# Right-side buffers on multiples of 64 bytes, later second halves of the first head, sooner block sums, recurrence chunks on alternating column groups

## The chip, the cores and the metric

The kernel runs on one core of one Trainium2 chip. The metric is the device time of one execution in microseconds (us); the times of several executions are given as a median.

## The reference, cut to what matters

One decoder layer over 1024 positions of width 1024, all in float32:

```python
mod = silu(c) @ w_ada + b_ada;  shift, scale, gate = split(mod, 3)
h = rmsnorm(x, norm_g) * (1 + scale) + shift
proj = h @ w_in                                   # 1024 x 8192
q_a, k_a, v_a, z_a, q_b, f_b, i_b, z_b, g_a, g_b = split(proj, cuts)
o_a = dilated_attention(q_a, k_a, v_a, rel_bias) * silu(z_a)       # 8 heads of 64
o_b = hgrn2_recurrence(silu(q_b), f_b, i_b, lb)                    # 8 heads of 128
o_b = rmsnorm(o_b, hgrn_onorm_g) * silu(z_b)
y = sigmoid(g_a) * (o_a @ w_branch_a) + sigmoid(g_b) * (o_b @ w_branch_b)
x = x + gate * (y @ w_out)
out = rmsnorm(x, final_g)
# recurrence, per head:  S_t = diag(f_t) S_{t-1} + (1 - f_t) i_t^T;  o_t = S_t^T q_t
```

The dilated attention is three patterns of distances merged by their softmax denominators; the kernel does it as one causal softmax whose bias depends on the distance alone, so one table row per head, read as a Toeplitz matrix, holds it.

## The kernel before, in words

**Products.** Every large matmul is done in triples: each operand is split in a rounded high part and the rest (`hi`, `lo`, names ending in h and l), and `mm3` (lines 239, 241, 240) adds hi x hi, lo x hi, hi x lo. The projection `h @ w_in` goes by 2 x 2 blocks of `h` (`b11`, `b12`, `b21`, `b22`) and block sums of them (`t1` to `t4`), seven products for a pair of column tiles in the place of eight; PSUM results are copied by ScalarE into `ct` tiles (`keep`, line 327, and the evictions `ev_...`), combined on VectorE, split, and stored to DRAM (`qk_d`, `vq_d`, ...) by DMAs on SyncE's queue (SP). `ct` is a pool of six buffers.

**Stages.** (1) Start: x is loaded, normalised and transposed, `mods` are made, `h` is written block by block (`make_h`, line 651 and 652), and the block sums are made (`block_sum`: a subtract on VectorE, line 674; a cast on ScalarE, line 675; the low part on VectorE, line 224). `tick` (line 680) moves every sum under way one step on and begins another. (2) A stream of projection steps. (3) Attention, eight heads; steps of the stream (`fill`) are put between its pieces so that TensorE has something to do while VectorE and ScalarE do the softmax. (4) Branch a's output product (`oah`, `oal`), (5) the recurrence, eight heads, again with stream steps between, (6) branch b, `w_out` and the last norm (`yh`, `yl`).

**Order.** TensorE's order is written by hand everywhere, and in stage 1 and the first steps of 2 the other engines' too; later a scheduler orders the others. DMAs on GpSimd's queue (POOL) and on SP's are issued in program order of their engine.

**Attention of one head.** `load_head` (line 865) loads from `qk_d` the first 512 positions of `qp`, `k1`, `k2` (`load_half(h, 0)`), the Toeplitz table `toep` (128 x 1024, 512 KB) and the first half of `vq` (`load_value`); after the second score the other halves follow (`load_half(h, 1)`). `score` makes a row block of 128 queries: two matmuls into `pss` (lines 903, 904), VectorE adds the bias and finds the maximum (line 906), ScalarE takes the exponential, VectorE scales (line 911). `turn` transposes the result on TensorE (`pt`, line 921), `value` multiplies with `vq` (line 936). For head 0 two scores (`begin(0)`) are made before the first `turn`.

**Recurrence of one head.** Levels of chunks `hl` = 1, 2, ..., 64: pairs of neighbouring chunks are joined by products `kk^T qq` into `pp`, which land in `amat`. At `hl` up to 16 (`small`, line 1094) every matmul has 32 stationary columns and writes one of four groups of 32 output partitions in turn. At `hl` = 32 (line 1113) sixteen matmuls write the groups 0 and 64 (+32) in turn; at `hl` = 64 (line 1122) eight matmuls all write partitions 0 to 63. ScalarE copies `pp` into `amat` (lines 1116 and 1124).

**Memory.** [...] At the right end the first tile put is `ctp`, so the small tiles there (of 2 or 8 floats) decide the start addresses of what follows: `ct`, the attention's buffers (`qp`, `k`, `toep`, `vq`, `s`, `pth`, `ptl`, `oa`), `oah`, `oal`, `b12`, `xt`, and the recurrence's (`qb`, `kk`, `amat`, `kt`, `yh`, `yl`, ...) start at 32 past a multiple of 64 bytes. `b11`, `b21`, `b22`, `t1` to `t4`, `w_hi`, `w_lo`, `w_raw` lie at the left end, at multiples of 64.

Of the kernel before, what the change touches and what calls it, by code (L numbers as in the profile page):

```python
# [10 lines left out]
F32 = mybir.dt.float32  # L11
# [8 lines left out]
P = 128  # L20
S = 1024
D = 1024
KT = D // P
# [156 lines left out]
def hybrid_layer(ctx: ExitStack, tc: tile.TileContext, x, w_ada, b_ada, w_in, w_branch_a, w_branch_b, w_out,  # L180
# [6 lines left out]
    dram = ctx.enter_context(tc.tile_pool(name="dram", bufs=1, space=DRAM))  # L187
    hctx = ctx.enter_context(ExitStack())
    hpool = hctx.enter_context(tc.tile_pool(name="hpool", bufs=1))
    cctx = ctx.enter_context(ExitStack())  # L190
    ctp = cctx.enter_context(tc.tile_pool(name="ctp", bufs=CT, side="right"))

# [322 lines left out]
    with ExitStack() as st:  # L515
# [1 line left out]
        pm = st.enter_context(tc.tile_pool(name="ps_main", bufs=1, space=PSUM))  # L517
        xt = [sp.tile([P, KT, 512], F32, name=f"xt{th}") for th in range(2)]
        add_blocks(sp, "b12")
        half = sp.tile([P, 2], F32, name="half")  # L520
        nc.gpsimd.memset(half, -0.5)
        scz = sp.tile([P, KT, 2, 32], F32, name="scz")
        nc.gpsimd.memset(scz, 0.0)
        sc = sp.tile([P, KT], F32, name="sc")
        nc.scalar.activation(half[:, 1:2], half[:, 1:2], AF.Sigmoid)
        nc.scalar.activation(sc, sm[:, C_C:C_C + KT], AF.Sigmoid)
        for a in range(2):
# [101 lines left out]
        def turn_late(j):  # L629

            ps = px.tile([P, 512], F32, name="pxt")
            for t in range(4):
                nc.tensor.transpose(ps[:, t * P:t * P + P], xs[4 + t][:, j * P:(j + 1) * P], ident)
            make_h(j, 1, ps)
# [39 lines left out]
            return [lambda: nc.vector.tensor_tensor(to, a, b_, ALU.subtract),  # L674
                    lambda: nc.scalar.copy(hi[:, s], to), lambda: sub(lo[:, s], to, hi[:, s])]

        sums = [(name, c) for name in ("t1", "t3", "t2", "t4") for c in range(2)]
        under_way = []

        def tick():  # L680

            if sums:
                under_way.append(block_sum(*sums.pop(0)))
            for parts in under_way:
                parts.pop(0)()
            while under_way and not under_way[0]:
                under_way.pop(0)
# [106 lines left out]
        first_products(2, (1,))  # L794
        tick()
        turn_late(3)
        first_products(3, (0,))
        mod_rows(2)
        first_products(3, (1,), (0,))
        mod_turn(2)  # L800
        for n in range(3, 6):
            split_first(n)
        first_products(3, (1,), (1,))
        mod_rows(3)
        first_products(3, (1,), (2,))
        mod_turn(3)
        tick()
        lx.close()
        add_blocks(hctx.enter_context(tc.tile_pool(name="hpool2", bufs=1, reuse_waits="tile")),
                   "b21", "b22", "t2", "t3")  # L810
        stream.issue()
        make_h(4, 0)
        turn_late(4)
        make_h(5, 0)
        first_products(4, (0,))
        turn_late(5)
# [42 lines left out]
    with ExitStack() as at:  # L859
# [7 lines left out]
        def load_head(h):  # L867
            p = h // 2
            if p > 0:
                stream.need(f"qk{p}")  # L870
            while turned.get(("v", p)) != 2:
                stream.step()
            qp, k1, k2 = ([ap1.tile([P, 512], F32R, name=f"{n}{c}") for c in range(2)] for n in ("qp", "k1", "k2"))
            toep = ap1.tile([P, S], F32, name="toep")
            heads[h] = qp, k1, k2, toep, [None, None]
            load_half(h, 0)
            nc.gpsimd.dma_start(toep, bass.AP(tensor=toep_d.tensor, offset=toep_d.offset + h * TOEP,
                                              ap=[[1, P], [1, S]]))
            load_value(h, 0)

        def load_half(h, c):
            qp, k1, k2, _, _ = heads[h]
            p, r = h // 2, slice(E * (h % 2), E * (h % 2) + E)
            for dst, n in ((qp, 4 * p), (k1, 4 * p + 2), (k2, 4 * p + 3)):
                for hh in range(2):
                    nc.gpsimd.dma_start(dst[c][E * hh:E * hh + E],
                                        qk_d[n + hh if dst is qp else n][r, half_of(c)].bitcast(F32R))
# [78 lines left out]
                value(*late.pop(0))  # L966

        load_head(0)
        fill.limit = in_gating
        fill.rate = (in_attention - stream.at) * 4 / NH / sum((j + 1) * w for j, w in enumerate(ATT_W))  # L970
        fill(2.0)
        for _ in begin(0):
            fill(0.5)
        for n, (h, j) in enumerate(items):
            nxt = begin(n + 1)
            for m in range(j + 1):
# [61 lines left out]
    with ExitStack() as hg:  # L1038
# [3 lines left out]
        pools["t"] = hg.enter_context(tc.tile_pool(name="ps_tr", bufs=1, **again))  # L1042
        pou = hg.enter_context(tc.tile_pool(name="ps_ou", bufs=2, **again))

        half = g1.tile([P, 8], F32, name="halfh")
        nc.gpsimd.memset(half, -0.5)
        am = g1.tile([P, 8, P], F32, name="amat")
        nc.gpsimd.memset(am, 0.0)
# [32 lines left out]
        def recurrence(h):  # L1081
# [17 lines left out]
            while hl < P:  # L1099
                q4 = qq.rearrange("p (n two t) -> p n two t", two=2, t=hl)  # L1100
                k4 = kk.rearrange("p (n two t) -> p n two t", two=2, t=hl)
                t3 = fq[:, :2 * n].rearrange("p (n two) -> p n two", two=2)
                if hl <= 16:
                    pl = small(2 if hl == 1 else 1)
                    if hl == 1:
                        nc.vector.tensor_tensor(d3, pl[:, :, 0], mask(0), ALU.mult)
                    nc.vector.copy_predicated(d3, mask(1 + LEVELS.index(hl)).bitcast(I32), pl[:, :, 1 if hl == 1 else 0])
                elif hl == 32:
                    pl = pp.tile([P, 512], F32, name="pp")[:, :256]
                    for c in range(8):  # L1110
                        for b in range(2):
                            o = c * P + 64 * b
                            nc.tensor.matmul(pl[64 * b:64 * b + 32, c * 32:c * 32 + 32], kk[:, o:o + 32],
                                             qq[:, o + 32:o + 64], start=True, stop=True)
                    for b in range(2):
                        nc.scalar.copy(am[64 * b:64 * b + 32, :, 64 * b + 32:64 * b + 64],
                                       c3(pl[64 * b:64 * b + 32]))
                else:
                    pl = pp.tile([P, 512], F32, name="pp")
                    for c in range(8):  # L1120
                        o = c * P
                        nc.tensor.matmul(pl[0:64, c * 64:c * 64 + 64], kk[:, o:o + 64], qq[:, o + 64:o + P],
                                         start=True, stop=True)
                    nc.scalar.copy(am[0:64, :, 64:P], c3(pl[0:64]))
                k_end = t3[:, :, 1:2].to_broadcast([P, n, hl])
                nc.vector.tensor_tensor(k4[:, :, 0, :], k4[:, :, 0, :], k_end, ALU.mult)
                q_end = t3[:, :, 0:1].to_broadcast([P, n, hl])
                nc.vector.tensor_tensor(q4[:, :, 1, :], q4[:, :, 1, :], q_end, ALU.mult)
                if fq is tot:
                    tn = g1.tile([P, S // 2], F32, name="totn")  # L1130
                    other = tot, tn
                else:
                    tn = other[0] if fq is other[1] else other[1]
                nc.vector.tensor_tensor(tn[:, :n], t3[:, :, 0], t3[:, :, 1], ALU.mult)
                fq = tn
                n //= 2
                hl *= 2
                yield 2.6
                if hl == 8:
                    load_z(h)  # L1140
                if hl == 32 and h + 1 < NHB:
                    load_f(h + 1)
# [84 lines left out]
    with ExitStack() as mg:  # L1227
# [122 lines left out]
        with ExitStack() as fo:  # L1350
            f1 = fo.enter_context(tc.tile_pool(name="fo1", bufs=1, **right))
            f2 = fo.enter_context(tc.tile_pool(name="fo2", bufs=2, **right))
            half = f1.tile([P, 1], F32, name="halff")
            nc.gpsimd.memset(half, -0.5)
            fg = f1.tile([P, D], F32, name="fg")
            nc.sync.dma_start(fg, final_g.to_broadcast([P, D]))
# [103 lines left out]
```

## Time and profile before

| | |
|---|---|
| median of 3 runs | 1141.77 us (1139.42 to 1144.51) |
| the profiled execution, its own time | 1141.97 us |
| its span in the trace | 1140.2 us |
| mean granted TensorE clock over the span | 0.994 |
| TensorE busy | 1112.2 us, 98% |
| VectorE / ScalarE / GpSimd busy | 71% / 45% / 10% |

The profiled execution lies 0.2 us from the median. A busy TensorE is one with a matmul in flight; a matmul's start and its length overlap with the next one's, so the distance from one start to the next is what a matmul costs.

### The profile page before, as it was taken

What the parts mean: (1) busy time and instruction counts of PE and PEld (TensorE: products, weight loads), DVE (VectorE), ACT (ScalarE), POOL (GpSimd) and SP (SyncE); (2) the same over time, 40 slices, a digit from 0 to 9 for tenths busy, and PEclk for the clock granted to TensorE, in tenths of its full rate; (3) what the DMA queues carried; (4) which work ended last, traced back from release to release, by engine and by line L of the source; (5) the groups of instructions that cost most, each with busy time, mean ns of one, the idle gap of its engine ahead of it and who ended that gap; (6) DMA issues with size and microseconds to landing.
All of it is one profiled execution on the core that took longest, in us unless ns stands there. A gap on an engine that the chain in (4) does not pass through costs nothing.

```text
span 1140.2 us, 21715 instructions
## 1 busy us (share of the span) xinstructions
PE 1112.2 (98%) x8322; PEld 912.8 (80%) x8322; DVE 808.2 (71%) x1607; ACT 516.5 (45%) x1056; POOL 117.2 (10%) x195
## 2 busy tenths in 40 slices
PE   7998999999999999999999999999999999999997
PEld 5677788888888888878887878787887878888886
DVE  4486888878877776844778797878888773769053
ACT  4474555677555555632343444333443432334021
POOL 1102112202202201100000000000000012000000
PEclk9999999999999999999999999999999999999999
DMA  9739476656646624856625254443535379864052
GB/s 321 219 102 252 136 195 181 180 131 163 153 120 162 158 80 139 265 174 195 222 89 173 93 168 140 141 155 107 174 90 181 106 252 328 276 209 140 21 184 74
DMA packets 161480, 189.54 MB, mean 166 GB/s; under 512 B 11312, under 2 KB 107696, under 8 KB 161376
## 3 DMA queue, kind: packets, MB, share of 16 engines
q1 hardware_dynamic: 140080, 153.95, 42.3%
q0 software_dynamic: 20896, 33.60, 12.2%
q8 instruction: 65, 1.06, 0.4%
q10 hardware_dynamic: 400, 0.61, 0.2%
q14 instruction: 39, 0.32, 0.1%
HBM read 129.36 MB, written 58.76 MB: 165 GB/s over the span
## 4 chain that ended last, share of the span: by engine, by line
PE 85%; DVE 6%; DMA 4%; issue 2%; ACT 2%; POOL 1%; SPq 0%; POOLq 0%; DVEq 0%; ACTq 0%
PE m L239 18%; PE m L241 17%; PE m L240 16%; PE pq L240 4%; PE pq L241 4%; PE pq L239 4%; PE po L936 3%; PE pt L921 3%; PE pp L1094 3%; PE pss L904 2%; PE pss L903 1%; PE pou L1177 1%; PE pou L1162 1%; PE pou L1179 1%; PE pxt L640 1%
## 5 line engine op out<-in xcount | busy, mean ns | idle before, releaser
L224 DVE TENSOR_TENSOR w_lo<-w_raw,w_hi 128x512 fp32r<-128x512 f32 x156 | 106.7, 687 | 54.1 <-ACT w_hi L246 48.6
L246 ACT CAST w_hi<-w_raw 128x512 fp32r<-128x512 f32 x146 | 90.5, 620 | 59.9 <-PE m L241 50.3
L327 ACT COPY ct<-m 128x512 f32<-128x512 f32 x90 | 52.6, 585 | 93.7 <-PE m L241 72.0
L246 ACT CAST w_hi<-w_s 128x512 fp32r<-128x512 f32 x90 | 55.9, 621 | 74.0 <-PE m L241 51.0
L274 DVE TENSOR_TENSOR ct<-m,ct 128x512 f32<-128x512 f32 x90 | 61.8, 686 | 26.5 <-PE m L241 26.1
L224 DVE TENSOR_TENSOR w_lo<-w_s,w_hi 128x512 fp32r<-128x512 f32 x90 | 61.8, 687 | 15.2 <-ACT w_hi L246 13.5
L909 ACT ACTIVATE s<-s,st 128x128 f32<-128x128 f32 (+3 forms) x64 | 49.8, 778 | 31.5 <-DVE st L906 31.4
L925 ACT CAST pth<-pt 128x512 fp32r<-128x512 f32 (+1 forms) x80 | 43.6, 544 | 36.5 <-PE pt L921 32.0
L224 DVE TENSOR_TENSOR ptl<-pt,pth 128x512 fp32r<-128x512 f32 (+1 forms) x80 | 50.5, 631 | 7.7 <-ACT pth L925 7.0
L239 PE MATMUL m<-t2h,w_hi 128*128 128x512 f32 x120 | 50.4, 420 | 4.2 <-ACT ct L327 4.2
L1185 POOL TENSOR_TENSOR ssh<-ssh,halfh 128x4 f32<-128x4 f32 x16 | 18.1, 1128 | 345.1 <-DVE ssh L1184 345.1
L239 PE MATMUL m<-b11h,w_hi 128*128 128x512 f32 x124 | 51.6, 416 | 0.0
L239 PE MATMUL m<-b21h,w_hi 128*128 128x512 f32 x124 | 51.2, 413 | 0.0
L239 PE MATMUL m<-b22h,w_hi 128*128 128x512 f32 x124 | 50.8, 410 | 0.0
L239 PE MATMUL m<-t1h,w_hi 128*128 128x512 f32 x120 | 50.3, 419 | 0.5 <-DVE ct L274 0.5
L239 PE MATMUL m<-t4h,w_hi 128*128 128x512 f32 x120 | 49.6, 414 | 0.4 <-DVE ct L274 0.4
L239 PE MATMUL m<-t3h,w_hi 128*128 128x512 f32 x120 | 49.6, 414 | 0.0
L241 PE MATMUL m<-b11l,w_hi 128*128 128x512 f32 x124 | 48.8, 394 | 0.0
L241 PE MATMUL m<-b21l,w_hi 128*128 128x512 f32 x124 | 48.7, 393 | 0.0
L241 PE MATMUL m<-b22l,w_hi 128*128 128x512 f32 x124 | 48.7, 393 | 0.0
L240 PE MATMUL m<-b11h,w_lo 128*128 128x512 f32 x124 | 48.5, 391 | 0.0
L240 PE MATMUL m<-b21h,w_lo 128*128 128x512 f32 x124 | 48.5, 391 | 0.0
(358 smaller groups left out, 3193.8 us busy)
## 6 DMA issues: line engine op xcount, KB each, us to landing
w_raw<-in_w_in_dram SPq DMA_DIRECT2D x128, 256.0 KB, 3.4
wa<-in_w_ada_dram SPq DMA_DIRECT2D x16, 512.0 KB, 8.9
qk_d<-ct SPq DMA_DIRECT2D x32, 256.0 KB, 3.5
k<-qk_d POOLq DMA_DIRECT2D x64, 128.0 KB, 4.9
qp<-qk_d POOLq DMA_DIRECT2D x32, 128.0 KB, 4.9
toep<-toep_d POOLq DMA_DIRECT2D x8, 512.0 KB, 6.5
vq_d<-ct SPq DMA_DIRECT2D x16, 256.0 KB, 3.4
vq<-vq_d POOLq DMA_DIRECT2D x16, 256.0 KB, 4.2
```

The lines of the kernel that those rows point to most:

```text
L224: nc.vector.tensor_tensor(out_, a, hi.bitcast(F32), ALU.subtract)
L239: nc.tensor.matmul(ps, ah, bh, start=start, stop=False, skip_group_check=more)
L240: nc.tensor.matmul(ps, al, bh, start=False, stop=False, skip_group_check=more)
L241: nc.tensor.matmul(ps, ah, bl, start=False, stop=stop, skip_group_check=more)
L246: nc.scalar.copy(hi, src)
L274: nc.vector.tensor_tensor(out_, a, b_, op)
L327: nc.scalar.copy(c[name], b[which])
L909: nc.scalar.activation(s[:, :kw], s[:, :kw], AF.Exp, bias=prev, scale=-1.0, accum_out=st2[:, 2:3])
L921: nc.tensor.transpose(pt[:, c0:c0 + P], pn[b][:, kt * P:(kt + 1) * P], ident)
L925: nc.scalar.copy(pth[:, :w], pt[:, :w])
L936: nc.tensor.matmul(po[:, 256 - n:256], vq[kt // 4][:, kt % 4], src[:, c0:c0 + n], start=kt == 0 and a == 0, stop=kt == 2 * j + 1 and a == 1)
L1094: nc.tensor.matmul(pl[32 * b:32 * b + 32, c], kk[:, o:o + 32], qb[:, 2 - n:2, o:o + 32], start=True, stop=True)
```

## The change

1. A tile of 8 floats, `edge`, is put at the right end ahead of everything, and the small tiles `half`, `sc`, `halfh`, `halff` become 16 floats. The tiles named under Memory then start at multiples of 64 bytes.
2. `toep` is loaded in two halves of 512 columns, each with its `load_half`. For head 0, four copies of one column from the first `vq` tile into the second halves' tiles stand ahead of their loads, so that these are issued after that `vq` has landed.
3. The block sums come in another order, and `tick` is called at other places.
4. The first two scores of head 0 are made sooner in TensorE's order.
5. At `hl` = 32 and 64 neighbouring chunks write different groups of output partitions (four groups, two groups), and the copies to `amat` become four of 32 x 128 and two of 64 x 256.

```diff
+    ctx.enter_context(tc.tile_pool(name="edge", bufs=1, side="right")).tile([P, 8], F32, name="edge")
     ctp = cctx.enter_context(tc.tile_pool(name="ctp", bufs=CT, side="right"))
...
-        sums = [(name, c) for name in ("t1", "t3", "t2", "t4") for c in range(2)]
+        sums = [("t1", 0), ("t1", 1), ("t3", 0), ("t2", 0), ("t3", 1), ("t2", 1), ("t4", 0), ("t4", 1)]
...
-        def tick():
+        def tick(another=True):
-            if sums:
+            if sums and another:
...
         turn_late(3)
+        tick()
         first_products(3, (0,))
...
         mod_turn(2)
+        tick(False)
...
         mod_turn(3)
-        tick()
...
         turn_late(4)
+        tick(False)
...
             load_half(h, 0)
-            nc.gpsimd.dma_start(toep, bass.AP(tensor=toep_d.tensor, offset=toep_d.offset + h * TOEP,
-                                              ap=[[1, P], [1, S]]))
             load_value(h, 0)
...
+            if h == 0 and c == 1:
+                got = heads[h][4][0][:, 0, 0:1].bitcast(F32)
+                for t in (qp[1], k1[1], k2[1]):
+                    nc.gpsimd.tensor_copy(t[:, 0:1], got)
+                nc.gpsimd.tensor_copy(toep[:, 512:513], got)
+            nc.gpsimd.dma_start(toep[:, half_of(c)],
+                                bass.AP(tensor=toep_d.tensor, offset=toep_d.offset + h * TOEP + 512 * c,
+                                        ap=[[1, P], [1, 512]]))
...
         load_head(0)
+        first = begin(0)
...
-        fill(2.0)
-        for _ in begin(0):
-            fill(0.5)
+        for amount in (0.7, 2.3):
+            next(first)
+            fill(amount)
+        next(first, None)
...
-                    pl = pp.tile([P, 512], F32, name="pp")
-                    for c in range(8):
-                        o = c * P
-                        nc.tensor.matmul(pl[0:64, c * 64:c * 64 + 64], kk[:, o:o + 64], qq[:, o + 64:o + P],
-                                         start=True, stop=True)
-                    nc.scalar.copy(am[0:64, :, 64:P], c3(pl[0:64]))
+                    for c in range(8):
+                        for o in range(0, P, 2 * hl):
+                            to = o + hl * (c % 2)
+                            nc.tensor.matmul(pl[to:to + hl, c // 2], kk[:, c * P + o:c * P + o + hl],
+                                             qq[:, c * P + o + hl:c * P + o + 2 * hl], start=True, stop=True)
+                    pairs = am.rearrange("p (c two) t -> p two c t", two=2)
+                    for odd in range(2):
+                        for o in range(0, P, 2 * hl):
+                            nc.scalar.copy(pairs[o:o + hl, odd, :, o + hl:o + 2 * hl],
+                                           pl[o + hl * odd:o + hl * odd + hl])
```

GpSimd's queue at head 0, before the change: the loads of `qp`, `k` (k1 and k2), `toep` and `vq` (`vq_d` is written by the stream).

```order
L886 DMA qp_1007<-qk_d 64x512 x2
L886 DMA k_1009<-qk_d 64x512 x2
L886 DMA k_1011<-qk_d 64x512 x2
L877 DMA toep<-toep_d 128x1024
L886 DMA qp_1008<-qk_d 64x512 x2
L886 DMA k_1010<-qk_d 64x512 x2
L886 DMA k_1012<-qk_d 64x512
L891 DMA vq<-vq_d 128x4x128
L886 DMA k_1012<-qk_d 64x512
L891 DMA vq<-vq_d 128x4x128 x2
```

The same place of the changed kernel:

```order
L891 DMA toep<-toep_d 128x512
L897 DMA qp_1011<-qk_d 64x512 x2
L897 DMA k_1013<-qk_d 64x512 x2
L897 DMA k_1015<-qk_d 64x512 x2
L902 DMA vq<-vq_d 128x4x128 x3
L889 CAST qp_1012<-vq 128x1
L889 CAST k_1014<-vq 128x1
L889 CAST k_1016<-vq 128x1
L890 COPY toep<-vq 128x1
L891 DMA toep<-toep_d 128x512
L897 DMA qp_1012<-qk_d 64x512 x2
L897 DMA k_1014<-qk_d 64x512 x2
```

Ahead of the first `vq` stood eleven loads of `qp` and `k` and the whole `toep`; now there stand six and half a `toep`, and the second halves have moved behind the `vq` loads and the four copies.

ScalarE in stage 1, around the casts of `t1`'s two halves (`row` feeds the transposes of `mods`; `b21h` is a block that TensorE reads next), before:

```order
L652 CAST b12h<-xt_114 128x512
L577 COPY row<-pmod 128x256
L609 CAST w_hi<-w_raw_321 128x512
L609 CAST w_hi<-w_raw_323 128x512
L609 CAST w_hi<-w_raw_325 128x512
L577 COPY row<-pmod 128x256
L675 CAST t1h<-xt_113 128x1024
L651 ACTIVATE xt_113<-xt_113,mods 128x512
L652 CAST b21h<-xt_113 128x512
```

and of the changed kernel:

```order
L654 CAST b12h<-xt_118 128x512
L677 CAST t1h<-xt_117 128x1024
L579 COPY row<-pmod 128x256
L677 CAST t1h<-xt_117 128x1024
L611 CAST w_hi<-w_raw_325 128x512
L611 CAST w_hi<-w_raw_327 128x512
L611 CAST w_hi<-w_raw_329 128x512
L579 COPY row<-pmod 128x256
L653 ACTIVATE xt_117<-xt_117,mods 128x512
L654 CAST b21h<-xt_117 128x512
```

Both casts of `t1h` now stand ahead of the three `w_hi`; none stands between the second `row` and `b21h`.

TensorE at the start of attention, from the second score of head 0 to the first transposes of a softmax (`pt`, line 921), before; the first score stands 8 rows further up:

```order
L903 MATMUL pss<-k_1009,qp_1007 128x256
L904 MATMUL pss<-k_1011,qp_1007 128x256
L239 MATMUL m_888<-t3h,w_hi 128x512
L240 MATMUL m_888<-t3h,w_lo 128x512
L241 MATMUL m_888<-t3l,w_hi 128x512
L239 MATMUL m_888<-t3h,w_hi 128x512
L240 MATMUL m_888<-t3h,w_lo 128x512
L241 MATMUL m_888<-t3l,w_hi 128x512
L921 MATMUL pt<-kc,s_1061 128x128
L921 MATMUL pt<-kc,s_1082 128x128 x2
```

and in the changed kernel, the rows around the two scores:

```order
L243 MATMUL m_912<-b22l,w_hi 128x512
L914 MATMUL pss<-k_1013,qp_1011 128x128
L915 MATMUL pss<-k_1015,qp_1011 128x128
L241 MATMUL m_912<-b22h,w_hi 128x512
L242 MATMUL m_912<-b22h,w_lo 128x512
L243 MATMUL m_912<-b22l,w_hi 128x512
L241 MATMUL m_912<-b22h,w_hi 128x512
L242 MATMUL m_912<-b22h,w_lo 128x512
L243 MATMUL m_912<-b22l,w_hi 128x512
L914 MATMUL pss<-k_1013,qp_1011 128x256
L915 MATMUL pss<-k_1015,qp_1011 128x256
L241 MATMUL m_912<-b22h,w_hi 128x512
```

Between the second score and the first `pt` there are now 27 matmuls of 512 columns in the place of 6; the `pt` rows stand where they stood, and elsewhere TensorE's order is the same.

## Rows read from the trace of the kernel before

**Rows 1.** The page: busy time of each engine.

```profile
PE 1112.2 (98%) x8322; PEld 912.8 (80%) x8322; DVE 808.2 (71%) x1607; ACT 516.5 (45%) x1056; POOL 117.2 (10%) x195
```

**Rows 2.** Timeline of PE, 95 to 106 us: start, length, instruction, idle before and releaser.

```profile
96.48 1.03 PE L447 MATMUL pt<-kc,ct 128*128 128x128 f32 x8
101.68 0.78 PE L239 MATMUL m<-t2h,w_hi 128*128 128x512 f32 x1 [4.16 <-ACT ct L327]
...
105.20 0.39 PE L241 MATMUL m<-t2l,w_hi 128*128 128x512 f32 x1
105.43 0.39 PE L239 MATMUL m<-t2h,w_hi 128*128 128x512 f32 x1
```

**Rows 3.** Windows: us, PE, PEld, DVE, ACT, POOL busy, then PEclk, DMA share, GB/s.

```profile
97.00:101.60 4.60, 0.52 (x5) 0.28 (x3) 1.16 (x2) 0.56 (x2) 0.00 (x0) 1.00 1.05 305
101.60:105.20 3.60, 3.52 (x9) 2.79 (x9) 2.98 (x6) 1.95 (x6) 2.84 (x4) 0.53 0.57 123
```

**Rows 4.** Timeline of ACT, 95 to 106 us.

```profile
101.04 0.59 ACT L327 COPY ct<-m 128x512 f32<-128x512 f32 x1 [4.29 <-DMA vq_d<-ct]
```

**Rows 5.** Timeline of POOL's issues, 84 to 106 us.

```profile
89.00 0.58 POOL L877 DMA_DIRECT2D toep<-toep_d  x1
...
102.11 0.79 POOL L891 DMA_DIRECT2D vq<-vq_d  x1 [9.95 <-ACT ct L327]
```

**Rows 6.** The page's DMA issues: KB each, median us from issue to landing.

```profile
k<-qk_d POOLq DMA_DIRECT2D x64, 128.0 KB, 4.9
...
toep<-toep_d POOLq DMA_DIRECT2D x8, 512.0 KB, 6.5
vq_d<-ct SPq DMA_DIRECT2D x16, 256.0 KB, 3.4
vq<-vq_d POOLq DMA_DIRECT2D x16, 256.0 KB, 4.2
```

**Rows 7.** Timeline of SP's issues, 84 to 106 us.

```profile
94.22 11.49 SPq L453 DMA_DIRECT2D vq_d<-ct  x7
```

**Rows 8.** Timeline of PE, 59 to 62 us.

```profile
61.26 0.50 PE L661 MATMUL pm<-b21h,w_hi 128*128 128x512 f32 x1 [1.06 <-ACT b21h L652]
```

**Rows 9.** Timeline of ACT, 51 to 62 us.

```profile
54.61 0.37 ACT L577 COPY row<-pmod 128x256 f32<-128x256 f32 x1 [2.54 <-PE pmod L574]
...
58.79 1.05 ACT L675 CAST t1h<-xt 128x1024 fp32r<-128x1024 f32 x1
```

**Rows 10.** Timeline of PE, 109 to 125 us.

```profile
115.33 0.30 PE L921 MATMUL pt<-kc,s 128*128 128x128 f32 x1 [0.38 <-DVE s L911]
116.76 0.44 PE L921 MATMUL pt<-kc,s 128*128 128x128 f32 x2 [1.13 <-DVE s L911]
...
124.38 0.49 PE L903 MATMUL pss<-k,qp 128*128 128x512 f32 x1
```

**Rows 11.** Timeline of PE in the first recurrence head: blocks of small matmuls, two records each.

```profile
560.07 1.10 PE L1094 MATMUL pp<-qb,kk 128*32 128x64 f32 x64
...
564.04 0.76 PE L1094 MATMUL pp<-qb,kk 128*32 128x32 f32 x64
...
578.66 0.70 PE L1113 MATMUL pp<-qb,kk 128*32 128x32 f32 x32
...
581.55 1.15 PE L1122 MATMUL pp<-qb,kk 128*64 128x64 f32 x16
```

**Rows 12.** Groups by form on PE, 545 to 995 us: count, busy us, mean ns.

```profile
L241 PE MATMUL m<-b11l,w_hi 128*128 128x512 f32 x60 | 23.6, 394 | 0.0
...
L1122 PE MATMUL pp<-qb,kk 128*64 128x64 f32 x128 | 9.2, 225 | 0.0
```

**Rows 13.** Groups by form on PE, 480 to 560 us.

```profile
L239 PE MATMUL m<-oah,w_hi 128*128 128x512 f32 x64 | 25.5, 398 | 0.0
...
L239 PE MATMUL m<-t2h,w_hi 128*128 128x512 f32 x8 | 3.1, 389 | 0.0
```

**Rows 14.** Groups by form on PE, 990 to 1140 us.

```profile
L240 PE MATMUL pq<-t2h,yl 128*128 128x512 f32 x30 | 12.0, 399 | 0.0
```

More of the change, by code (lines that the diff above doesn't have):

```diff
@@ L519, in hybrid_layer @@
         add_blocks(sp, "b12")
-        half = sp.tile([P, 2], F32, name="half")
+        half = sp.tile([P, 16], F32, name="half")[:, 0:2]
         nc.gpsimd.memset(half, -0.5)
@@ L523, in hybrid_layer @@
         nc.gpsimd.memset(scz, 0.0)
-        sc = sp.tile([P, KT], F32, name="sc")
+        sc = sp.tile([P, 16], F32, name="sc")[:, 0:KT]
         nc.scalar.activation(half[:, 1:2], half[:, 1:2], AF.Sigmoid)
@@ L876, in load_head @@
             load_half(h, 0)
-            nc.gpsimd.dma_start(toep, bass.AP(tensor=toep_d.tensor, offset=toep_d.offset + h * TOEP,
-                                              ap=[[1, P], [1, S]]))
             load_value(h, 0)
         def load_half(h, c):
-            qp, k1, k2, _, _ = heads[h]
+            qp, k1, k2, toep, _ = heads[h]
+            if h == 0 and c == 1:
[6 more added lines that the diff above has]
+                                        ap=[[1, P], [1, 512]]))
             p, r = h // 2, slice(E * (h % 2), E * (h % 2) + E)
@@ L1043, in hybrid_layer @@
         pou = hg.enter_context(tc.tile_pool(name="ps_ou", bufs=2, **again))
-        half = g1.tile([P, 8], F32, name="halfh")
+        half = g1.tile([P, 16], F32, name="halfh")
         nc.gpsimd.memset(half, -0.5)
@@ L1107, in recurrence @@
                     nc.vector.copy_predicated(d3, mask(1 + LEVELS.index(hl)).bitcast(I32), pl[:, :, 1 if hl == 1 else 0])
-                elif hl == 32:
-                    pl = pp.tile([P, 512], F32, name="pp")[:, :256]
+                else:
+                    pl = pp.tile([P, 512], F32, name="pp")[:, :4 * hl].rearrange("p (c t) -> p c t", c=4)
                     for c in range(8):
[L1111 to L1118, printed above, removed]
-                    pl = pp.tile([P, 512], F32, name="pp")
-                    for c in range(8):
-                        o = c * P
-                        nc.tensor.matmul(pl[0:64, c * 64:c * 64 + 64], kk[:, o:o + 64], qq[:, o + 64:o + P],
-                                         start=True, stop=True)
-                    nc.scalar.copy(am[0:64, :, 64:P], c3(pl[0:64]))
+                        for o in range(0, P, 2 * hl):
[7 more added lines that the diff above has]
+                                           pl[o + hl * odd:o + hl * odd + hl])
                 k_end = t3[:, :, 1:2].to_broadcast([P, n, hl])
@@ L1352, in hybrid_layer @@
             f2 = fo.enter_context(tc.tile_pool(name="fo2", bufs=2, **right))
-            half = f1.tile([P, 1], F32, name="halff")
+            half = f1.tile([P, 16], F32, name="halff")[:, 0:1]
             nc.gpsimd.memset(half, -0.5)
```

## The prediction

> **What bounds the kernel now.** The first view is the page's busy times [rows 1]: TensorE has a matmul in flight for 1112.2 of 1140.2 us, so there are two ways to gain, its gaps (28 us in all) and the cost of what it runs. The second view is the timeline of TensorE, where a bracket names a wait. The longest one that the change touches is at 101.68 us: 4.16 us idle, for a copy into a `ct` tile on ScalarE [rows 2]. [...] After that wait the matmuls start further apart: the eight from 101.68 to 105.20 took 3.52 us, where the next one starts 0.23 us after its forerunner. [...] Following the wait back: ScalarE's copy at 101.04 stood still for 4.29 us until a store of `vq_d` had left its `ct` tile [rows 4]; those stores begin to be issued on SP's queue at 94.22 [rows 7], so the first took some 6.8 us, against a median of 3.4 [rows 6]. In that stretch the DMA engines' share is 1.05 and they move 305 GB/s [rows 3]: the store is late because GpSimd's queue is loading all of head 0 beside it, the 512 KB of `toep` issued at 89.00 among it [rows 5]. Last come the views by form, for the lengths of single matmuls.
>
> **The change part by part.** The sum is made against the profiled execution, 1141.97 us, which is 0.2 us above the median.
>
> *Later loads.* Before, eleven loads of `qp` and `k` at 128 KB and a `toep` of 512 KB [rows 6] stand ahead of the first `vq`: 1.9 MB. After, six and half a `toep`: 1.0 MB. With half the load the queue is empty before the stores begin, and I give the store its median: issued at 94.22, landed at 97.6, copied by 98.3 with the 0.59 us of [rows 4]. TensorE runs dry at 97.5 (the row at 96.48 and its 1.03 us), so 0.8 us remain of 4.16, and a wait that short leaves the clock alone: the matmul behind the wait of 1.06 us at 61.26 lasts 0.50 us [rows 8], the one behind 4.16 us 0.78 [rows 2]. The slow matmuls lost 3.52 less 8 x 0.23, 1.7 us. **Gain 3.4 + 1.7, 5.0 us.** Bounds: 0, if the store is late for another reason, and 5.8.
>
> Where the stall goes: the second halves are late next. `vq` is issued when its store has landed, now near 99 us and not 102.11 [rows 5]; at 4.2 us to landing [rows 6] the four copies behind it begin near 103.5. No row prices such a copy; at 0.58 us, the length of an issue [rows 5], they and the seven loads behind them take 6.4 us of GpSimd, and the last load lands, at 4.9 us [rows 6], near 115. The first score that reads a second half stands at 124.38 [rows 10], which the gains ahead of it bring to about 117. They have 2 us to spare; the cost is nothing unless they are later than that, and then what they are later (bounds 0 and 3, at copies of 1 us and loads as slow as the 6.5 us of `toep`). Behind those loads on GpSimd's queue stand only the loads of head 1, due a head later. The other heads' `toep` in two halves is one more issue of some 0.5 us each on a GpSimd that is 10% busy [rows 1]: nothing.
>
> *Sooner sums.* TensorE waits 1.06 us at 61.26 for `b21h` [rows 8], and on ScalarE a cast of `t1h`, 1.05 us, stands ahead of it at 58.79 [rows 9]. It moves up to where ScalarE idled 2.54 us before 54.61 [rows 9]. The other half's cast now stands ahead of the three `w_hi` casts and may push these by 1 us. **Gain 0.9 us**, bounds a loss of 1 and a gain of 1.06. The later sums are named by no wait of TensorE.
>
> *Sooner scores.* The two first transposes of a softmax wait 0.38 and 1.13 us for VectorE's scaling [rows 10]. Ahead of them there were 6 matmuls behind the second score; now there are 27, at 0.23 us 6.2 us of work. **Gain 1.5 us**, bounds 0 and 1.5. What the scores read, the first halves, is issued by the time at which `toep` was before, 89.00, and takes at most the 6.5 us of the whole `toep`: there before 100, when the score comes.
>
> *Column groups.* This is arithmetic on four blocks of the first recurrence head [rows 11]. At 64 columns, sixteen records in one group take 1.15 us, and 64 records in four groups 1.10 us. At 32 columns, 32 records in two groups take 0.70 us, and 64 in four groups 0.76 us. So it isn't the records that cost but the rounds, a round being one matmul in each group: all four blocks have sixteen. With a last matmul of 0.22 us [rows 12], a round is (1.15 - 0.22) / 15, 0.062 us, and (0.76 - 0.22) / 15, 0.036 us. The change makes eight rounds of each: 7 x 0.062 + 0.22 is 0.65 us (0.50 less) and 7 x 0.036 + 0.22 is 0.47 us (0.23 less). I take 0.71 a head for the drain between blocks, over eight heads. **Gain 5.7 us.** Bounds: 0, if groups of 64 and four of 32 at this step don't overlap, and 7.4, if all of 1.15 and 0.70 were halved. [...]
>
> The copies into `amat` become six a head, three more. Each is at most as long as a copy of 512, 0.59 us [rows 4], on an engine 45% busy [rows 1]; ScalarE also makes the `w_hi` that the stream waits for. Bounds 0 and 14 us (24 copies); I take **a loss of 1.0 us**, as if two heads held the stream up by one copy each.
>
> *Alignment.* Of matmuls with 512 columns beside each other, those on `oah` (at 32 past a multiple of 64) last 398 ns, those on `t2h` (at a multiple) 389 [rows 13]; those on `yl` 399 [rows 14]. There are 192 on `oah` and `oal`, 30 on `yl`: 222 x 9 ns, **a gain of 2.0 us**. Bounds: 0, if something else in those rows differs, and some 10 us above that: in the recurrence a matmul with both operands aligned lasts 394 [rows 12], 5 ns over the 389 of the quiet stage, and nothing in the rows says whether the traffic of the misaligned `ct` causes it; 7 products of 3 groups of 60 there and about as many in attention make some 2,400 x 4 ns. I stay with the row that names the tile. [...]
>
> **Sum:** 5.0 + 0.9 + 1.5 + 5.7 - 1.0 + 2.0 = 14.1 us, so 1141.97 - 14.1 = 1127.9.
>
> **The rivals.**
> A. The stall stays: the store is late by the stream's own weight loads, or another `ct` is. For it: a share of 1.05 leaves no room, and it isn't only GpSimd's queue. Against it: GpSimd's part halves. 1127.9 + 5.0 = 1133.
> B. The groups don't overlap in this step. For it: no row shows two groups of 64. Against it: groups of 32 do [rows 11]. 1127.9 + 5.7 = 1133.6. A and B together: 1138.6, no change.
> C. Alignment gives nothing: 1130. Its opposite, C', is that it also frees the aligned matmuls of stages 3 and 5: 1118.
> D. The slower side: going from one column group to another costs, rather than overlaps. Eight heads x (8 + 16) matmuls make 192 such changes. The rest of the sum is a gain of 8.4 us, so from 44 ns each the gain is gone, and from 73 ns each the kernel is slower by 5.7: 1148 at that. For it: a round of 64 columns costs 62 ns alone, so a wait for the end of one of 225 [rows 12] would do it. Against it: blocks with four groups change with every matmul and cost no more.
>
> **How the numbers follow.** What a measurement tells from no change is about 0.5%, 5.7 us. The forecast as summed has 0.45 (1125 to 1131), C 0.15, C' 0.12, A 0.12, B 0.09, A with B 0.04, D 0.03. Leaving out half of C' below, and A with B and D above, the range is 1119 to 1135. Faster by over 0.5% is below 1136: all but the last two and a tail of A and B, 0.84; no change 0.12; slower 0.04.
>
> **What would show it.** Right: the row on `t2h` behind the eight transposes with under 1 us idle and 0.23 us to the next; no wait for `b21h` at 61; none at the first `pt`; blocks of line 1127 of about 0.47 and 0.65 us; `oah` and `yl` at 389. Wrong: a wait of TensorE or VectorE on GpSimd's loads at the fifth score (late second halves), new waits for `w_hi` behind line 1132 in the recurrence, or blocks of 0.7 and 1.15 us as before.

## The result and the profile after

The changed kernel takes 1131.03 us (median of 6 runs, 1129.33 to 1134.70) against 1142.15 of the kernel before (6 runs): a ratio over all these runs of 0.9909, 95% interval 0.9895 to 0.9924, which is 10.4 us less (the two medians by themselves lie 11.1 us apart). The profiled execution took 1134.70 us (span 1132.9) and is the slowest of the six; two of its waits (2.50 and 2.05 us) were shorter when the same kernel was profiled again (0.95 and 0.47 us).

The page's busy times, and TensorE's timeline at the places of [rows 2], [rows 8], [rows 10] and [rows 11]:

```profile
PE 1105.6 (98%) x8322; PEld 908.8 (80%) x8322; DVE 807.6 (71%) x1607; ACT 519.5 (46%) x1080; POOL 123.1 (11%) x207
```

```profile
59.36 0.50 PE L663 MATMUL pm<-b21h,w_hi 128*128 128x512 f32 x1
...
94.57 1.03 PE L449 MATMUL pt<-kc,ct 128*128 128x128 f32 x8
96.73 0.50 PE L241 MATMUL m<-t2h,w_hi 128*128 128x512 f32 x1 [1.13 <-ACT ct L329]
97.07 0.40 PE L242 MATMUL m<-t2h,w_lo 128*128 128x512 f32 x1
...
108.33 0.49 PE L932 MATMUL pt<-kc,s 128*128 128x128 f32 x3
...
115.99 0.48 PE L914 MATMUL pss<-k,qp 128*128 128x512 f32 x1
...
122.17 0.50 PE L914 MATMUL pss<-k,qp 128*128 128x512 f32 x1 [2.50 <-DVE st L917]
...
474.34 0.75 PE L241 MATMUL m<-b11h,w_hi 128*128 128x512 f32 x1 [2.05 <-DVE ct L276]
...
577.07 0.46 PE L1127 MATMUL pp<-qb,kk 128*32 128x32 f32 x32
...
579.73 0.69 PE L1127 MATMUL pp<-qb,kk 128*64 128x64 f32 x16
```

The reader is to see what has gone and what has come. Gone: the wait for `b21h`, the two waits at the first `pt`, 3.0 of the 4.16 us on `t2h` (and the slow clock behind: from 97 to 101 us it is granted 1.00, where behind the wait before it was 0.53 [rows 3], and the next matmul starts 0.34 us later, at 97.07, not 0.58), 0.24 and 0.46 us of the two blocks of the recurrence. Come: 2.50 us at 122.17, where a score waits for VectorE. The row at 115.99, the first to read a second half, has no bracket: the late loads are in time. What they do is seen in ScalarE's timeline and in the windows (columns as in [rows 3]):

```profile
117.62 0.59 ACT L329 COPY ct<-m 128x512 f32<-128x512 f32 x1 [3.32 <-DMA qk_d<-ct]
```

```profile
89.00:92.00 3.00, 3.00 (x16) 2.52 (x15) 2.24 (x4) 2.01 (x6) 0.00 (x0) 1.00 0.41 77
101.00:122.00 21.00, 18.67 (x88) 15.19 (x86) 16.12 (x38) 10.62 (x24) 5.12 (x13) 1.00 0.99 265
...
122.00:126.00 4.00, 3.70 (x13) 2.87 (x14) 2.98 (x11) 2.28 (x5) 0.00 (x0) 0.60 0.41 131
```

A copy into `ct` stands still for 3.32 us again, now under a store of `qk_d`; behind it on ScalarE is a `w_hi`, behind that VectorE's `w_lo`, which stands still for 3.25 us until 118.76, and behind that, in VectorE's order, the score's reduction, at 121.42. From 101 to 122 us the DMA engines' share is 0.99: the second halves (1.0 MB) lie there now, beside weights and stores, while from 89 to 92 us the share is 0.41. Behind the wait the granted clock falls to 0.60. The wait at 474 is behind a load of `ga_d`.

The form rows that answer to [rows 13] and [rows 14]:

```profile
L241 PE MATMUL m<-oah,w_hi 128*128 128x512 f32 x64 | 25.3, 396 | 0.0
L242 PE MATMUL m<-oah,w_lo 128*128 128x512 f32 x64 | 25.3, 395 | 0.0
L243 PE MATMUL m<-oal,w_hi 128*128 128x512 f32 x64 | 25.3, 395 | 0.0
```

```profile
L241 PE MATMUL pq<-t2h,yh 128*128 128x512 f32 x30 | 11.9, 397 | 0.0
L243 PE MATMUL pq<-t2l,yh 128*128 128x512 f32 x30 | 11.8, 394 | 0.0
L242 PE MATMUL pq<-t2h,yl 128*128 128x512 f32 x30 | 11.8, 394 | 0.0
```

Aligned, `oah` still lasts 396 ns and not 389; `yl` went from 399 to 394.

### The profile page after: what moved, and what is told of

Same layout as the page of the kernel before. It is cut to its first block, busy times and chain, and to the rows that moved or that the text cites. A ratio compares the mean times of both kernels' runs of the same rounds, so it can differ in the third digit from the quotient of the medians.

```text
span 1132.9 us, 21754 instructions
## 1 busy us (share of the span) xinstructions
PE 1105.6 (98%) x8322; PEld 908.8 (80%) x8322; DVE 807.6 (71%) x1607; ACT 519.5 (46%) x1080; POOL 123.1 (11%) x207
## 3 DMA queue, kind: packets, MB, share of 16 engines
q8 instruction: 65, 1.06, 0.4%
## 4 chain that ended last, share of the span: by engine, by line
PE 88%; DVE 4%; DMA 3%; ACT 2%; issue 1%; POOL 1%; POOLq 0%; DVEq 0%; ACTq 0%; SPq 0%
PE m L241 18%; PE m L243 16%; PE m L242 16%; PE pq L243 5%; PE pq L242 5%; PE pq L241 5%; PE po L947 3%; PE pt L932 3%; PE pp L1107 3%; PE pss L915 1%; PE pss L914 1%; PE pou L1186 1%; DMA w_raw<-in_w_in_dram 1%; PE pou L1188 1%; PE pm L663 1%
```

## The experiments

The theory after the result: the gain is that of the column groups, the sums and the scores; alignment gives little, and the later loads pay with a new wait for what they take off the old one. The rivals: alignment carries several us all over the kernel; the new wait belongs to the sooner scores; it is a chance of one execution. Ten runs have times enough for an interval; each ratio is to runs of the kernel before beside it (medians 1140.55 to 1142.29):

| run | median, us | ratio to before, 95% interval |
|---|---|---|
| column groups alone | 1136.89 | 0.9957 (0.9942 to 0.9972) |
| sums and scores alone | 1136.81 | 0.9949 (0.9930 to 0.9968) |
| alignment alone | 1140.76 | 0.9989 (0.9972 to 1.0006) |
| later loads alone | 1140.68 | 0.9995 (0.9983 to 1.0008) |
| changed, without alignment | 1135.77 | 0.9931 (0.9904 to 0.9958) |
| changed, old loads | 1130.44 | 0.9893 (0.9874 to 0.9912) |
| changed, again | 1129.93 | 0.9906 (0.9890 to 0.9923) |
| changed, toep and qp at once | 1128.86 | 0.9902 (0.9880 to 0.9924) |
| the same again | 1130.33 | 0.9898 (0.9877 to 0.9918) |
| changed, toep, qp and k1 at once | 1130.45 | 0.9910 (0.9888 to 0.9931) |

The four parts alone multiply to 0.9890; the whole is 0.9909. What the parts give alone is about what they give together.

**Column groups alone.**

```diff
-                        nc.tensor.matmul(pl[0:64, c * 64:c * 64 + 64], kk[:, o:o + 64], ...)
+                            to = o + hl * (c % 2)
+                            nc.tensor.matmul(pl[to:to + hl, c // 2], kk[:, c * P + o:c * P + o + hl], ...)
```

> The kernel before with only the column groups of the recurrence changed (hl = 32 and 64 on alternating groups, six copies). Theory: rounds set the price, blocks of 0.39 and 0.61 us in the place of 0.63 and 1.07, eight heads, so 5.6 us less than before, about 1136.5; the stall of 4.2 us at 101.7 us is still there. Rival: part of what the changed kernel gained in the recurrence came from the buffers' alignment there; then this run gains less than 4.

0.9957 of 1141.48 is 4.9 us (3.2 to 6.6). The timeline of TensorE has the same two blocks as in the changed kernel, with the buffers as before:

```profile
577.44 0.46 PE L1114 MATMUL pp<-qb,kk 128*32 128x32 f32 x32
577.83 0.50 PE L239 MATMUL m<-b22h,w_hi 128*128 128x512 f32 x1
...
580.09 0.69 PE L1114 MATMUL pp<-qb,kk 128*64 128x64 f32 x16
580.71 0.50 PE L239 MATMUL m<-b21h,w_hi 128*128 128x512 f32 x1
```

(The expectation's 0.39 and 0.61 are the distances from a block's first start to the next row's start; the savings are the same by either measure.) So the blocks owe nothing to alignment: 0.24 and 0.46 us less than [rows 11], 5.6 us over eight heads. The whole recurrence says the same: from the first matmul into `pp` to the last it is 372.7 to 372.9 us in the four profiles with the old groups and 367.1 to 367.4 in the nine with alternating ones.

**The same groups without alternation.**

```diff
-                            to = o + hl * (c % 2)
-                            nc.tensor.matmul(pl[to:to + hl, c // 2], ...)
+                            to = o + hl * (c // 4)
+                            nc.tensor.matmul(pl[to:to + hl, c % 4], ...)
```

> The changed kernel, with the same column groups and the same six copies in the recurrence, but neighbouring chunks on the same groups: chunks 0 to 3 on the first, 4 to 7 on the second. Theory (a round is what matmuls on different groups do at once): without alternation sixteen rounds are back, blocks of about 0.63 us at 32 columns and 1.07 at 64. Rival (the price hangs on the count of groups or on the copies, or the engine looks further ahead than its next matmul): blocks of 0.39 and 0.61 us as in the changed kernel.

Neither the theory nor the rival holds. Timed once, 1137.51 us; the timeline, and windows of 0.28, 0.21 and 0.36 us over the 64-column block (PE and PEld busy with the count of records, then clock):

```profile
575.56 0.60 PE L1127 MATMUL pp<-qb,kk 128*32 128x32 f32 x32
...
578.36 0.97 PE L1127 MATMUL pp<-qb,kk 128*64 128x64 f32 x16
```

```profile
578.35:578.63 0.28, 0.27 (x4) 0.27 (x5) 1.00 0.00 0
578.63:578.84 0.21, 0.21 (x11) 0.21 (x9) 1.00 0.00 0
578.84:579.20 0.36, 0.36 (x12) 0.35 (x8) 1.00 0.00 0
```

0.97 lies between 1.15 and 0.69, 0.60 between 0.70 and 0.46. The counts (records in flight in each window) say how: few in the first window, most in the second. There the last records of the first group run beside the first of the second; at both ends one group runs alone. The single records of the trace bear this out: each group has eight, most of them 58 ns apart, and the second group's first starts 0.29 us into the block, beside the first group's fifth. Here matmuls of different groups did overlap without standing next to each other, but only from 0.29 us into the block; alternation is worth the rest, 0.28 of the 0.46 us and 0.14 of the 0.24.

**Sums and scores alone.** The diff's parts on `sums`, `tick`, `begin(0)`; loads, buffers and recurrence as before.

```diff
-        sums = [(name, c) for name in ("t1", "t3", "t2", "t4") for c in range(2)]
+        sums = [("t1", 0), ("t1", 1), ("t3", 0), ("t2", 0), ("t3", 1), ("t2", 1), ("t4", 0), ("t4", 1)]
...
+        first = begin(0)
```

> The kernel before with only the sooner block sums and the sooner first scores, which lie far enough apart to be read separately in one trace. Theory: no wait for b21h near 61 us (0.95 us), none at the first transposes of a softmax (1.9 us), the wait of 4.2 us near 101 us as before: 2.5 us less, 1138.5. Rival: the sooner scores bring a wait of their own near 122 us and the sum is nothing, 1141.

5.8 us less (3.7 to 8.0), twice what was expected. TensorE's timeline:

```profile
59.03 0.50 PE L661 MATMUL pm<-b21h,w_hi 128*128 128x512 f32 x1
...
96.78 0.50 PE L239 MATMUL m<-t2h,w_hi 128*128 128x512 f32 x1 [1.50 <-ACT ct L327]
...
108.32 0.49 PE L923 MATMUL pt<-kc,s 128*128 128x128 f32 x3
```

The two small waits are gone as expected, and no wait follows at 122, which takes the rival away. But in this profile the wait on `t2h` is 1.50 us and no slow clock follows it (granted 1.00 from 96 to 105 us), with the old loads all in place.

**Old loads in the changed kernel.**

```diff
-            nc.gpsimd.dma_start(toep[:, half_of(c)], ...)      # in load_half
+            nc.gpsimd.dma_start(toep, ...)                     # in load_head
```

> The changed kernel with head 0's loads as they were (toep whole, second halves ahead of the first vq). Theory: the wait of about 4 us for a ct tile comes back near 97 us, with the slow clock behind it (5 us in all), and the wait near 122 us (0.9 to 2.5 us in the changed kernel, with up to 1.3 us of slow clock) is gone, so 1 to 4 us more than the changed kernel, 1131 to 1134. Rival (the wait near 122 us belongs to the sooner scores): it is there too, 1135 or more.

The wait is back, and the one at 122 is gone; the time is that of the changed kernel (1130.44 against 1131.03 and 1129.93), a little under what was expected:

```profile
99.98 0.50 PE L241 MATMUL m<-t2h,w_hi 128*128 128x512 f32 x1 [3.50 <-ACT ct L329]
```

```profile
100.00:105.00 5.00, 5.00 (x23) 4.17 (x24) 3.95 (x8) 2.75 (x7) 2.85 (x4) 1.00 0.78 174
```

After 3.50 us idle the granted clock stayed at 1.00; after 4.16 it fell to 0.53 [rows 3]. The two other profiles with the old loads, column groups alone and then alignment alone, have shorter waits than 4.16 and a fall behind each:

```profile
99.92 0.59 PE L239 MATMUL m<-t2h,w_hi 128*128 128x512 f32 x1 [3.84 <-ACT ct L327]
98.83 0.50 PE L241 MATMUL m<-t2h,w_hi 128*128 128x512 f32 x1 [3.09 <-ACT ct L329]
```

```profile
100.00:105.00 5.00, 5.00 (x15) 3.96 (x16) 4.01 (x8) 2.69 (x7) 2.86 (x4) 0.66 0.73 152
100.00:105.00 5.00, 5.00 (x17) 3.92 (x16) 4.02 (x9) 1.60 (x5) 2.11 (x4) 0.67 0.97 201
```

So of five waits with the old loads three have a slow clock behind them (4.16, 3.84 and 3.09 us; granted 0.67, 0.66 and 0.67 from 100 to 105 us) and two don't (3.50 and 1.50; granted 1.00 behind them): in these traces the length of the wait alone doesn't decide it.

The traces also show why moving the loads gives nothing in all. The second profile of the changed kernel (below) has 2.1 us less from the first matmul on `b21h` to the one on `t2h` above than this run (37.67 against 39.75), 1.8 us more from the first score matmul of 512 columns to the eleventh (21.60 against 19.83), and 0.57 us more at the very end: from the last matmul on `yh` to the end of the span it is 6.84 to 6.85 us in the five profiles that load `toep` whole and 7.41 to 7.43 in the nine that load it in halves. What causes these 0.57 us wasn't looked into.

**Later loads alone.**

```diff
-            nc.gpsimd.dma_start(toep, ...)
+            if h == 0 and c == 1:
+                got = heads[h][4][0][:, 0, 0:1].bitcast(F32)
+                for t in (qp[1], k1[1], k2[1]):
+                    nc.gpsimd.tensor_copy(t[:, 0:1], got)
```

> The kernel before with only the later loads of head 0's second halves. Theory: the wait of 4.2 us at 101.7 us falls to about 1 us and the slow clock behind it goes, 5 us in all at that place, but a wait of 2 to 3 us for a ct tile under a store of qk_d comes up near 125 us, so 1 to 4 us less than before in all, 1138 to 1141. Rival: the new wait comes from the sooner scores, not from the loads; then it isn't seen here and the run gives 5, 1137.

0.6 us less, an interval that holds nothing. The wait on `t2h` fell, but the new wait came elsewhere than the theory said, at the first `pt`, where it was 0.38 us before [rows 10]:

```profile
97.28 0.50 PE L239 MATMUL m<-t2h,w_hi 128*128 128x512 f32 x1 [1.86 <-ACT ct L327]
...
111.01 0.30 PE L928 MATMUL pt<-kc,s 128*128 128x128 f32 x1 [2.03 <-DVE s L918]
112.44 0.44 PE L928 MATMUL pt<-kc,s 128*128 128x128 f32 x2 [1.13 <-DVE s L918]
```

```profile
104.02 0.59 ACT L327 COPY ct<-m 128x512 f32<-128x512 f32 x1 [2.30 <-DMA vq_d<-ct]
105.16 0.69 DVE L224 TENSOR_TENSOR w_lo<-w_raw,w_hi 128x512 fp32r<-128x512 f32 x1 [2.11 <-ACT w_hi L246]
```

It is the same cause one station earlier: ScalarE waits 2.3 us at 104 for a store of `vq_d`, `w_hi` is late, VectorE waits 2.1 us for it with the first softmax behind. In the changed kernel the sooner scores give the softmax more time, no wait stands at the first `pt`, and the next late store, of `qk_d`, shows (3.32 us of ScalarE at 117.62).

**The changed kernel again.**

> The changed kernel once more, unaltered. Theory (the stretch from 101 to 121 us is now short of DMA bandwidth): a wait of TensorE of 1 to 3 us behind the sixth score near 122 us is there again, from a ct tile or a piece of weights that is late; 1131. Rival (a chance of the one execution that was profiled): no such wait. The wait of 2.0 us near 474 us, behind a load of ga_d, was 0.5 us in the kernel before; if it is chance, it is under 1 us here.

```profile
PE m L241 <- ACT ct L329: 1.4, 1, 1.4
PE pss L914 <- DVE st L917: 0.9, 1, 0.9
```

In these waits of TensorE (90 to 135 us) the one near 122 is there again, smaller and without a fall of the clock (0.95 us, granted 1.00 from 121 to 126 us); the one at 474 is 0.47 us. In the other twelve profiles the longest wait of TensorE from 462 to 495 us is 0.4 to 1.8 us, so the 2.05 is the top of a spread; it is 0.7 us on average in the five profiles of the kernel before and its variants and 1.3 in the nine of the changed kernel and its variants, and whether the change adds to it was not tried. The five profiles with the sooner scores and all second halves held back have a wait near 122 us, of 2.5, 0.9, 1.5, 1.0 and 0.3 us: no chance of one execution, though its size is.

**toep and qp at once, only k1 and k2 held back.**

```diff
-                for t in (qp[1], k1[1], k2[1]):
+                for t in (k1[1], k2[1]):
                     nc.gpsimd.tensor_copy(t[:, 0:1], got)
-                nc.gpsimd.tensor_copy(toep[:, 512:513], got)
```

> The changed kernel, but of head 0's second halves only k1 and k2 are held back behind vq; the second half of toep and qp (0.38 MB) is loaded at once, into the stretch from 90 to 92 us in which the changed kernel's DMA engines stand idle. Theory (bandwidth from 101 to 121 us): the wait near 122 us shrinks by the time of 0.38 MB at 300 GB/s, 1.3 us, and the slow clock behind it may go as well, so 1 to 3 us less than the changed kernel, 1128 to 1130; the wait at 97 us stays at about 1 us. Rival: the early loads push the first stores of vq_d, the wait at 97 us grows to 2 us or more, and the time is that of the changed kernel or above.

> Once more the changed kernel with toep's and qp's second halves loaded at once and only k1 and k2 held back. The run before gave 1128.86 against 1129.93 for the changed kernel beside it, too near to be told apart, though the wait near 122 us was gone. Theory: gone again, 1127 to 1130. Rival (it was chance): a wait of about 1 us there, 1130 to 1131.

By the rows, what is loaded at once is 0.5 MB and not the expectation's 0.38: half a `toep` is 256 KB, and `qp` is two loads of 128 KB [rows 6]. TensorE's waits from 90 to 135 us of the first of the two profiles, and two windows:

```profile
PE m L241 <- ACT ct L329: 1.2, 1, 1.2
```

```profile
89.00:92.00 3.00, 3.00 (x15) 2.48 (x14) 2.56 (x5) 1.53 (x5) 1.01 (x2) 1.00 1.07 229
101.00:122.00 21.00, 21.00 (x104) 17.55 (x103) 19.05 (x47) 13.25 (x30) 3.15 (x6) 1.00 0.96 263
```

The gap of the DMA engines is filled (1.07 in the place of 0.41), the wait near 122 is gone in both, and TensorE is busy for all 21 us. From the first score matmul of 512 columns to the eleventh the two profiles have 19.70 and 19.72 us, the changed kernel's two 24.30 and 21.60. The mechanism is shown; the gain in the time isn't: 0.9902 and 0.9898 against 0.9906 are one and the same within their intervals.

**k1 at once too.**

```diff
-                for t in (k1[1], k2[1]):
-                    nc.gpsimd.tensor_copy(t[:, 0:1], got)
+                nc.gpsimd.tensor_copy(k2[1][:, 0:1], got)
```

> As the run with toep and qp at once, with k1 (another 0.13 MB at each of two loads' halves, 0.51 MB in all at once) as well; only k2 is held back. Theory: 0.5 us better than that run at most if the early loads are over by 92.3 us, when the stores of vq_d begin; else the wait at 97 us grows by what they are late. Rival: as there.

No better (0.8 MB at once by the rows, where the expectation says 0.51). The wait near 122 is gone here too; the wait on `t2h` is 2.3 us and the granted clock behind it, from 100 to 105 us, 0.66, as the rival has it for early loads that reach into the stores of `vq_d`; one profile, so that cause is argued, not shown. No version tried beats the changed kernel by more than can be told.

**Alignment alone, and the changed kernel without it.**

```diff
+    ctx.enter_context(tc.tile_pool(name="edge", bufs=1, side="right")).tile([P, 8], F32, name="edge")
...
-        half = sp.tile([P, 2], F32, name="half")
+        half = sp.tile([P, 16], F32, name="half")[:, 0:2]
```

> The kernel before with only the edge tile and the small tiles of 16 floats. Theory (the rows of the changed kernel, where matmuls on oah still last 396 ns): alignment to 64 bytes gives nothing that can be measured, 1141 to 1142. Rival: it frees the traffic of the ct tiles as well, 1136 or less.

> The changed kernel without the edge tile and with the small tiles as they were. Theory: as the changed kernel, 1131 to 1132, the recurrence's blocks at 0.39 and 0.61 us. Rival (alignment carries part of the gain): 1134 or more.

Alone it gives 1.3 us (a loss of 0.7 to a gain of 3.2). Without it the median is 4 us up, as the rival said, but its five times stand in two bunches, two at 1129.7 and 1130.2, three at 1135.8 to 1136.5, and the profiled one (1135.9) lost 2.6 us before 61 us, with the clock at 0.90 up to 24 us, where the changed kernel has 1.00:

```profile
0.00:24.00 24.00, 19.96 (x134) 14.66 (x134) 10.05 (x27) 10.56 (x18) 3.81 (x12) 0.90 0.97 300
```

The run without alternation has 0.90 there as well, and it is aligned; so that is no effect of alignment. Behind the start, the rows of scores of 512 columns from 200 to 400 us are without alignment and with it:

```profile
L913 PE MATMUL pss<-k,qp 128*128 128x512 f32 x29 | 11.4, 394 | 0.0
```

```profile
L915 PE MATMUL pss<-k,qp 128*128 128x512 f32 x29 | 11.3, 391 | 0.0
```

Three ns of 394, and 1 to 2 ns of 398 on `oah`. The times can't tell so little from nothing, but the traces can, for stretches of TensorE in which no wait differs take the same time in every profile. From the start of the first matmul named to that of the last, in us:

| stretch | 5 profiles without alignment | 8 with it | edge of 24 |
|---|---|---|---|
| scores of 512 columns, eleventh to last | 288.92 to 288.96 | 288.39 to 288.42 | 288.20 |
| on `oah` and `oal` | 44.82 | 44.48 | 43.82 |
| on `yh` and `yl` | 55.49 | 55.17 | 55.35 |

The three make 1.2 us, close to the 1.3 that alignment alone gave. The recurrence shows nothing: with the old groups it is 372.70 to 372.92 us in three profiles without alignment and 372.76 with it.

**An edge of 24 floats.**

```diff
-.tile([P, 8], F32, name="edge")
+.tile([P, 24], F32, name="edge")
```

> The changed kernel with an edge tile of 24 floats in the place of 8: the right end's tiles start 64 bytes lower, at multiples of 64 still. If what counts is the multiple of 64, matmuls on oah and oal read as in the changed kernel (395 to 396 ns, with the same spread from one to the next), those on yh 397 and on yl 394. If it is the two operands' addresses against each other at some other distance, these rows change, though the tiles stay aligned.

Timed once, 1127.96 us (the last column of the table above). The rows change although every tile is still at a multiple of 64 bytes:

```profile
L241 PE MATMUL m<-oah,w_hi 128*128 128x512 f32 x64 | 25.3, 395 | 0.0
L243 PE MATMUL m<-oal,w_hi 128*128 128x512 f32 x64 | 25.1, 392 | 0.0
L242 PE MATMUL m<-oah,w_lo 128*128 128x512 f32 x64 | 24.8, 388 | 0.0
```

So in this run the length of these matmuls moved with the address, by up to 7 ns (395 to 388), with the multiple of 64 kept. At what distance, and of which operands, wasn't tried. 1127.96 isn't read as a gain: the wait near 122 is 0.3 us in it and its start is 1.1 us quicker, and both vary from run to run.

## Why the prediction was right, and where it wasn't

The time, 1131.03, lies in the range (1119 to 1135), and it is faster, as forecast; the 10.4 us are 3.7 short of the sum of 14.1. Point by point:

*Column groups, 5.7 us:* right, 5.6 in the trace (0.24 and 0.46 a head against 0.23 and 0.50), 5.3 to 5.9 over the whole recurrence, 4.9 by the runs. Reading the price from rounds held for the alternating order. The two rows said nothing on groups whose matmuls don't alternate; the run without alternation showed that (0.60 and 0.97 us, with the second group's first record 0.29 us into the block of 64 columns).

*The copies, a loss of 1.0 us:* not seen. The blocks gave 5.6 and the whole recurrence, copies and all, was shorter by 5.3 to 5.9, so nothing near 1.0 was lost.

*Sums 0.9 and scores 1.5:* right in mechanism. The starts of the same matmul in two traces move by 0.95 us at 61 and by 1.9 at the first two `pt`; the second includes the gaps that a short wait leaves. The run of both alone gave 5.8; in its one profile the wait on `t2h` was 2.7 us shorter too and had no slow clock behind it (granted 1.00), which is enough to make up the difference, though one profile doesn't show that all its executions had it so.

*Later loads, 5.0 us:* this is the step that failed. The first half of it held: with the loads held back the wait was 1.1 us (0.8 forecast). Three things were missing. The 4.16 us were the longest of what the old loads give: the five profiles with them have 4.2, 3.8, 3.1, 3.5 and 1.5, mean 3.2, the six with them held back 1.1, 1.4, 0.9, 0.9, 1.9 and 1.7, mean 1.3; so 1.9 us and not 3.4. The slow clock, 1.7 of the 5.0 (granted 0.53 behind the wait [rows 3]), doesn't follow from the wait's length in these traces, as the prediction had it from two waits (1.06 us without, 4.16 with): with the old loads three of five profiles have it (0.66 or 0.67 from 100 to 105 us), and with the loads held back it came behind other waits, of 2.50 us near 122 in the changed kernel (granted 0.60 from 122 to 126 us), of 2.03 and 1.13 at the first `pt` in the run of later loads alone (granted 0.66 from 113 to 118 us), and of 1.54 near 124 in the run without alignment (granted 0.66 from 124 to 129 us). And the moved 0.9 MB landed where the DMA engines had no room (a share of 0.99 from 101 to 122 us): the prediction asked whether the second halves would be late (they weren't), not whom they would make late. Rival A, "the store is late ... or another `ct` is", named that wait and priced the whole at 1133; it holds in its second half, with `qk_d` and at 122 us. By the run with old loads, the net of the part is nothing. That the total still came near the sum is in part luck: this term fell out almost whole, and the copies that cost nothing and the scores' 0.4 us more made up for some of it.

*Alignment, 2.0 us:* right in sign, 1.2 in size, wrong in reason. `oah` fell by 2 ns and not 9 (and only a third of its 192 matmuls had lasted 398, the others 396), `yl` by 5, while the two groups on `yh` rose (from 394 and 391 to 397 and 394); nearly half of the 1.2 us is the scores', for which the prediction had no term. That `t2h` lasts 389 and `oah` 396 isn't alignment to 64: both are aligned in the changed kernel, and these are its numbers.

*Rivals B, C', D* fell: groups of 64 overlap, stage 3 gained 0.5 us by alignment and stage 5 nothing, and changing groups costs nothing that shows (0.46 and 0.69 us for the blocks that change with every matmul, 0.70 and 1.15 before). C (alignment nothing, 1130) can't be told from the time, but the stretches of the traces speak against it.

What stays open: whether the sooner sums shorten the wait on `t2h` (1.50 in their run with old loads, 3.50 in the changed kernel with old loads) or whether both are draws from the same spread; what else than a wait's length decides whether the clock falls behind it (0.67 after 3.09 us, 1.00 after 3.50); and which operand distance sets the length of the matmuls on `oah`.

## What to carry to other kernels

Here loads that were moved out of the way of one store (TensorE's wait on `t2h` fell from 4.16 to 1.13 us) were in the way of the next (3.32 us of ScalarE behind `qk_d`, 2.50 us of TensorE): before a transfer is moved, read the DMA share of the stretch that it moves into (0.99 here from 101 to 122 us), and whether an idle one lies nearer (0.41 from 89 to 92 us). One profile's wait was one draw, of 1.5 to 4.2 us in five profiles with the same loads; a term that is read from a DMA wait or from a slow clock needs a second profile before it goes into a sum at full size. Small matmuls of different column groups ran beside each other here (0.69 us for a block in the place of 1.15), so write neighbouring ones to different groups; that was worth about as much as the sooner sums and scores together (4.9 and 5.8 us, each alone).

## What was not expected of the hardware

Matmuls that use all 128 rows but write different groups of output partitions ran at the same time even when half of them stood together (0.97 us for a block that takes 1.15 in one group and 0.69 alternating). And the mean length of a 512-column matmul on `oah` moved with addresses 32 or 64 bytes apart, with both operands' shapes and types the same: with `w_lo` 396 ns before, 395 in the changed kernel and 388 with the edge of 24 floats, with `w_hi` 398, 396 and 395.
